# Weight sums of the seven-product units in a page of their own, and another order of the second run

## The chip, the cores and the metric

The kernel runs on one core of a Trainium2 chip. Five engines work side by side and wait for each other through semaphores: PE (TensorE: matmuls, and the loads of their stationary operand, PEld), DVE (VectorE), ACT (ScalarE), POOL (GpSimd) and SP (SyncE, which here issues most of the DMAs). The metric is the device time of one launch in microseconds (us). Lower is better.

## The reference

One layer of a hybrid encoder on 256 tokens of width 2048, in float32:

```
n = rms_norm(h); u = n @ W_in
a = MLA(u)                              (16 heads)
s = rms_norm((BiSSD(u)) * silu(z)) @ w_o_ssd       (K = 4096)
h = h + (sigmoid(g_a) * a + sigmoid(g_s) * s) @ W_out
h = h + (silu(gate) * val) @ ffn_w_down            (K = 5632), gate|val = conv(rms_norm(h) @ ffn_w_up)
out = rms_norm(h)
```

Two of its products matter here: that with `w_o_ssd` and that with `ffn_w_down`.

## The kernel before

**Jobs and half slabs.** All weights stream through one list of jobs. A job has a slab of 16 blocks of 128x128 (1 MB), loaded by one DMA into one of three `raw` buffers (L123; `load` is called two jobs ahead), and is used in half slabs. Since a float32 product is made of three products of rounded halves, each half slab is split: ACT copies it, rounded, into `wh` (L147, L190), and DVE subtracts that from the original into `wl` (L148, L191). There are five buffers of each (`HB=5`). Before PE uses half slab n, `ahead` (L1438) has `split_to` (L170) issue the splits through half slab n + 4, so splits run about five half slabs ahead of the matmuls.

**Seven-product units.** In most of the two products, two column groups, two token groups and two blocks of K form a 2x2 by 2x2 block product. Plain jobs take eight block products; a unit marked "seven" takes seven (`SEVEN`, L906), from sums of the activations (made once) and sums of the weights (made in the unit). With three matmuls of 512 columns each, a plain unit of the runs has 24 matmuls and a seven-product unit 21. A seven-product unit has four half slabs (`nh = 4`), and `split_seven` (L150) makes each of them:

- h = 0: B11 and B21, as they are;
- h = 1: T1 = B11 + B12 and T3 = B22 + B12, written over B11 and B12 in the slab (L159, L160), and then split;
- h = 2: T1 + B22 written over B11 (L163); B22 and that sum are split, each with its own copy and subtraction;
- h = 3: that sum + B21 written over B21 (L167), and then split (a half of the usual size).

So a seven-product unit has four adds of 128x512 on DVE and five copy/subtract pairs, two of 128x1024 and three of 128x512.

**Where they stand.** `os_run` (L916) makes the product with `w_o_ssd` in two runs, one for each half of the output columns; each run goes over 16 pairs of K blocks in an order that is written out by hand (L1331; S marks a seven-product unit): run 0 has four sevens, run 1 has six. At the end of a run, `inner` (L934) combines four of the sums after the last seven, and `outer` (L945) the rest. `mix_in` (L987) then gates and scales a run's result and adds it to the attention's part, which `mix_load` (L983) brings back from HBM; `mix_channels` (L994) transposes it on PE for the product with `W_out`. Those of run 0 are hung by `at(slot, ...)` to jobs of run 1 (L1346 to L1350): what hangs at a slot is issued before that job's matmuls. In the FFN, the first two of three parts of the down product have five seven-product units each, with a plain down job behind each (`L1384` to L1387).

**Order.** The text gives each engine's order only as a priority: the program is put into its final order when it is built, and an instruction that is ready may come before one that stands ahead of it in the text and is not. [...]

**Pages.** Larger intermediate tiles are pages of 4 KB per partition, from one pool of 29 (`page`, L77; `NPG=29`); a new page waits until one is free.

Of the kernel before, what the change touches and what calls it, by code (L numbers as in the profile page):

```python
# [15 lines left out]
P = 128  # L16
# [48 lines left out]
def tile_bidir_hybrid_layer(ctx: ExitStack, tc, xT, pos, vec, cst, w_in, w_r, w_v, w_qk, w_oa,  # L65
# [9 lines left out]
    act, dve, pe = nc.scalar, nc.vector, nc.tensor  # L75

    def page(shape, dt=F32, name="pg"):  # L77
        return pp.tile(shape, dt, tag="pg", bufs=NPG, name=name)
# [10 lines left out]
    def f32(ap):  # L89
        return ap.bitcast(F32)  # L90
# [55 lines left out]
    def hilo(wh, wl, v):  # L146
        act.activation(wh, v, AF.Copy)  # L147
        dve.tensor_sub(wl, v, f32(wh))  # L148

    def split_seven(i, h, wh, wl):  # L150


        r = raws[i].rearrange("p (m k) c -> p m k c", m=8)
        B11, B12, B21, B22 = r[:, :4, 0, :], r[:, 4:, 0, :], r[:, :4, 1, :], r[:, 4:, 1, :]
        if h == 0:
            vh, vl = (w.rearrange("p (k m) c -> p m k c", k=2) for w in (wh, wl))
            hilo(vh, vl, r[:, :4])
        elif h == 1:
            dve.tensor_add(B11, B11, B12)  # L159
            dve.tensor_add(B12, B22, B12)  # L160
            hilo(wh, wl, r[:, :, 0, :])
        elif h == 2:
            dve.tensor_add(B11, B11, B22)  # L163
            hilo(wh[:, :4, :], wl[:, :4, :], B22)
            hilo(wh[:, 4:, :], wl[:, 4:, :], B11)
        else:
            dve.tensor_add(B21, B11, B21)  # L167
            hilo(wh[:, :4, :], wl[:, :4, :], B21)

    def split_to(n):  # L170
        while hptr[0] < min(n, len(halves)):
            i, h, nb = halves[hptr[0]]
            wh = wp.tile([P, 8, P], F32R, tag="wh", bufs=HB, name="wh")
            wl = wp.tile([P, 8, P], F32R, tag="wl", bufs=HB, name="wl")
            if jobs[i].seven:
                split_seven(i, h, wh, wl)
                hl[hptr[0]] = (wh, wl)
                hptr[0] += 1
                continue
            if jobs[i].wide:  # L180
                r = raws[i].rearrange("p (m k) c -> p m k c", m=8)[:, 4 * h:4 * h + 4]
                vh, vl = (w.rearrange("p (k m) c -> p m k c", k=2) for w in (wh, wl))
            elif jobs[i].quad:

                r = raws[i].rearrange("p (m k) c -> p m k c", m=4)[:, :, 2 * h:2 * h + 2, :]
                vh, vl = (w.rearrange("p (k m) c -> p m k c", k=2) for w in (wh, wl))
            else:
                r = raws[i][:, 8 * h:8 * h + nb, :]
                vh, vl = wh[:, :nb, :], wl[:, :nb, :]
            act.activation(vh, r, AF.Copy)  # L190
            dve.tensor_sub(vl, r, f32(vh))  # L191
            hl[hptr[0]] = (wh, wl)
            hptr[0] += 1
# [793 lines left out]
    def mix_in(q, res):  # L987
        g = mixT[q] = mixS[q]
        for t in range(2):
            o = res[t, q % 2]  # L990
            dve.scalar_tensor_tensor(o, ts_[q][:, t, :], 1.0, o, ALU.add, ALU.mult)
            dve.scalar_tensor_tensor(g[:, t, :], o, r_ssd["t"][:, t:t + 1], g[:, t, :], ALU.mult, ALU.add)
# [212 lines left out]
    def at(slot, fn, *a):  # L1205
        late.append((slot, lambda: fn(*a)))
# [97 lines left out]
    for g in range(G):  # L1304
        b = len(jobs)
# [22 lines left out]
    b = len(jobs)  # L1328
    for g in range(G):
        at(b - 2 + g, ssd_split, g)  # L1330
    runs = "0 1 2 3 4 5 8 S10 9 S11 6 S14 7 S15 12 13", "0 1 2 3 4 S6 5 S7 8 S10 9 S11 12 S14 S15 13"  # L1331
    runs = [[(int(w.lstrip("S")), w[0] == "S") for w in r.split()] for r in runs]
    done = {}

# [10 lines left out]
    at(b + 17, ssd_r)  # L1345
    for q in range(2):  # L1346
        at(b + 17 + q, mix_load, q)
        at(b + 19 + q, lambda q: mix_in(q, done[0]), q)
        at(b + 20 + q, mix_channels, q)
        at(b + 25 + q, mix_load, 2 + q)  # L1350
    b = len(jobs)
    cells = [{} for _ in range(4)]
# [11 lines left out]
    b = len(jobs)  # L1364
# [115 lines left out]
    i = 0  # L1480
# [112 lines left out]
```

## Time and profile before

| | us |
|---|---|
| median of three runs | 1960.38 |
| lowest and highest run | 1959.31, 1964.65 |
| profiled execution | 1959.09 |
| its span, first to last instruction | 1957.3 |
| PE, PEld, DVE, ACT busy in the span | 1937.9, 1688.1, 1562.7, 1240.4 |
| mean granted clock of PE | 0.998 of full speed |

The runs of the product with `w_o_ssd` lie between 935 and 1117 us of the span, the seven-product units of the FFN between 1394 and 1454 and between 1660 and 1721 us.

A line of the timeline has the start, the duration, the engine, the line of the source, the operation, the tiles it writes and reads with their shapes, and a count where several were merged; square brackets hold the engine's idle time before it and what ended that. A row of the windows view has a stretch, its length, and the busy time and count of instructions of each engine, then PE's clock, the busy share of the DMA engines and GB/s. In the runs, the matmuls are at L931; in the FFN, those of the plain jobs at L217 and L224 and those of the sevens at L1098 to L1100.

### The profile page before, as it was taken

Reading aid. Unit: us, or ns where it says so; the run is one execution under the profiler, and the core shown is the slowest. Engines: PE = TensorE matmul, PEld = TensorE weight load, DVE = VectorE, ACT = ScalarE, POOL = GpSimd, SP = SyncE. Lnnn points to the kernel's source line nnn. Section 1 sums busy time; section 2 is a strip of 40 time slices with the busy share of each in tenths; the row PEclk is TensorE's granted clock in tenths of the full one; section 3 lists DMA queues with packets and bytes.
Section 4 is the critical chain, followed back from the end, with each engine's and each line's share of the span. In section 5 each row is a group of like instructions: output and inputs, shape, how many; then the busy total and the mean of one; then the engine's idle time right before and its main releaser. Section 6 shows DMA issues by size and latency. Waiting matters only on the chain.

```text
span 1957.3 us, 28870 instructions
## 1 busy us (share of the span) xinstructions
PE 1937.9 (99%) x10948; PEld 1688.1 (86%) x10948; DVE 1562.7 (80%) x2583; ACT 1240.4 (63%) x1975; POOL 16.2 (1%) x36
## 2 busy tenths in 40 slices
PE   9999999999999999999999999999999999999997
PEld 8899988888888888888878788888888888888887
DVE  8887765779879878879887886887887887887775
ACT  6566544778888988978554554656455565555563
POOL 0200000000000000000000000000000000000000
PEclk9999999999999999999999999999999999999999
DMA  7654457665565566565466575555456554464553
GB/s 287 199 166 147 141 175 222 240 234 171 201 234 191 195 217 205 186 216 189 153 212 213 168 265 183 183 178 209 160 175 225 178 209 173 172 215 173 202 169 124
DMA packets 118906, 379.55 MB, mean 194 GB/s; under 512 B 9712, under 2 KB 53168, under 8 KB 90864
## 3 DMA queue, kind: packets, MB, share of 16 engines
q1 hardware_dynamic: 116976, 375.09, 56.0%
q0 software_dynamic: 1024, 1.54, 0.3%
q8 instruction: 86, 1.41, 0.3%
q10 hardware_dynamic: 768, 1.09, 0.2%
q14 instruction: 52, 0.43, 0.1%
HBM read 372.08 MB, written 4.42 MB: 192 GB/s over the span
## 4 chain that ended last, share of the span: by engine, by line
PE 90%; DVE 6%; ACT 2%; DMA 1%; issue 1%; SPq 0%; ACTq 0%; DVEq 0%
PE g L217 39%; PE g L224 20%; PE g L931 6%; PE g L252 4%; PE g L253 4%; PE g L254 4%; DVE wl L191 2%; DVE wl L148 1%; PE s L931 1%; PE g L196 1%; PE g L198 1%; PE g L197 1%; ACT wh L190 1%; PE s L836 1%; PE s L845 1%
## 5 line engine op out<-in xcount | busy, mean ns | idle before, releaser
L191 DVE TENSOR_TENSOR wl<-raw,wh 128x1024 fp32r<-128x1024 f32 (+1 forms) x634 | 753.2, 1202 | 202.2 <-ACT wh L190 127.5
L190 ACT ACTIVATE wh<-raw 128x1024 fp32r<-128x1024 f32 (+1 forms) x634 | 651.4, 1038 | 276.4 <-PE g L217 102.2
L217 PE MATMUL g<-xHL,wh 128*128 128x512 f32 x1424 | 341.6, 392 | 0.2 <-DVE cu L267 0.2
L217 PE MATMUL g<-hHL,wh 128*128 128x512 f32 x1408 | 327.8, 390 | 0.0
L217 PEld LDWEIGHTS g<-xHL,wh 128*128 128x128 f32 x1424 | 262.5, 188 | 52.1 <-PE s L198 0.4
L217 PEld LDWEIGHTS g<-hHL,wh 128*128 128x128 f32 x1408 | 261.5, 188 | 52.4
L224 PEld LDWEIGHTS g<-xHL,wl 128*128 128x128 f32 x1424 | 182.6, 191 | 6.9
L224 PE MATMUL g<-xHL,wl 128*128 128x256 f32 x1424 | 184.7, 283 | 0.0
L224 PEld LDWEIGHTS g<-hHL,wl 128*128 128x128 f32 x1408 | 174.8, 192 | 3.4
L224 PE MATMUL g<-hHL,wl 128*128 128x256 f32 x1408 | 176.0, 283 | 0.0
L147 ACT ACTIVATE wh<-raw 128x512 fp32r<-128x512 f32 (+1 forms) x100 | 78.2, 798 | 101.5 <-DVE raw L160 53.5
L217 PE MATMUL g<-aHL,wh 128*128 128x512 f32 x532 | 129.2, 393 | 0.7
L1048 DVE SCALAR_TENSOR_TENSOR uc<-u,V,uc 128x255 f32<-128x255 f32 x176 | 84.9, 482 | 56.3 <-ACT uc L1046 54.6
L931 PE MATMUL g<-wh,yHL 128*128 128x512 f32 x392 | 125.6, 391 | 0.3 <-DVE m L948 0.3
L1046 ACT ACTIVATE uc<-u,V 128x256 f32<-128x256 f32 x88 | 52.3, 594 | 115.8 <-DVE u L274 115.8
L217 PEld LDWEIGHTS g<-aHL,wh 128*128 128x128 f32 x532 | 98.3, 188 | 24.5 <-ACT wh L190 4.2
L148 DVE TENSOR_TENSOR wl<-raw,wh 128x512 fp32r<-128x512 f32 (+1 forms) x100 | 88.5, 902 | 26.5 <-ACT wh L147 22.0
L252 PE MATMUL g<-wh,xHL 128*128 128x512 f32 x256 | 100.2, 391 | 0.0
L253 PE MATMUL g<-wl,xHL 128*128 128x512 f32 x256 | 99.9, 390 | 0.0
L254 PE MATMUL g<-wh,xHL 128*128 128x512 f32 x256 | 99.6, 389 | 0.0
L931 PEld LDWEIGHTS g<-wh,yHL 128*128 128x128 f32 x392 | 73.5, 188 | 16.0 <-issue 0.7
L931 PE MATMUL g<-wl,yHL 128*128 128x512 f32 x196 | 76.9, 393 | 1.3 <-DVE wl L191 1.3
(373 smaller groups left out, 2845.0 us busy)
## 6 DMA issues: line engine op xcount, KB each, us to landing
raw<-in_w_in SPq DMA_DIRECT2D x88, 1024.0 KB, 4.9
raw<-in_w_up SPq DMA_DIRECT2D x88, 1024.0 KB, 4.9
raw<-in_w_in SPq DMA_DIRECT2D x128, 256.0 KB, 3.8
raw<-in_w_os SPq DMA_DIRECT2D x32, 1024.0 KB, 6.1
raw<-in_w_dn SPq DMA_DIRECT2D x26, 1024.0 KB, 5.0
raw<-in_w_oa SPq DMA_DIRECT2D x64, 256.0 KB, 4.0
FB<-acsD SPq DMA_DIRECT2D x32, 512.0 KB, 7.8
raw<-in_w_out SPq DMA_DIRECT2D x12, 1024.0 KB, 6.0
```

The source lines that it names most:

```text
L147: act.activation(wh, v, AF.Copy)
L148: dve.tensor_sub(wl, v, f32(wh))
L190: act.activation(vh, r, AF.Copy)
L191: dve.tensor_sub(vl, r, f32(vh))
L217: pe.matmul(ps, lhsT=wh[:, b, :], rhs=x, start=k == 0, stop=False)
L224: pe.matmul(cell["ps"][:, 0, :], lhsT=wl[:, b, :], rhs=get(k)[:, 0, :], start=False, stop=k == ktot - 1)
L252: pe.matmul(ps, lhsT=x[:, 0, ts], rhs=wH[:, kk, :], start=k == 0, stop=False)
L253: pe.matmul(ps, lhsT=x[:, 0, ts], rhs=wL[:, kk, :], start=False, stop=False)
L254: pe.matmul(ps, lhsT=x[:, 1, ts], rhs=wH[:, kk, :], start=False, stop=k == kt - 1)
L931: pe.matmul(M[nm], lhsT=x, rhs=w, start=left[nm] == total[nm], stop=left[nm] == 1)
L1046: act.activation(o, u, AF.Identity, scale=vcol("fcw", 88 + cb), bias=vcol("fcb", cb))
L1048: dve.scalar_tensor_tensor(o[:, a], u[:, b], vcol("fcw", k * 88 + cb), o[:, a], ALU.mult, ALU.add)
```

## The change

`split_seven` makes T1 and T3 with the first half slab, behind its split, in a page of their own, `T13`. The second half slab is split from that page, through the same rearranged views of `wh` and `wl` as the first. Behind its split stand both running sums: T1 + B22 goes over B12, and that sum plus B21 over B21. The third and last half slabs are then split from the slab with no add of their own. The number of adds, copies and subtractions stays.

In run 1 the seven-product units stand between plain ones: S6 comes one place earlier, and 12 stands between S14 and S15. `mix_in` and `mix_channels` for run 0's result are hung one job earlier; `mix_load` stays.

```diff
+    sums = {}
+
     def split_seven(i, h, wh, wl):
...
         if h == 0:
             vh, vl = (w.rearrange("p (k m) c -> p m k c", k=2) for w in (wh, wl))
             hilo(vh, vl, r[:, :4])
+            t = sums[i] = page([P, 2, 4, P], name="T13")
+            dve.tensor_add(t[:, 0], B11, B12)
+            dve.tensor_add(t[:, 1], B22, B12)
         elif h == 1:
-            dve.tensor_add(B11, B11, B12)
-            dve.tensor_add(B12, B22, B12)
-            hilo(wh, wl, r[:, :, 0, :])
+            t = sums.pop(i)
+            vh, vl = (w.rearrange("p (k m) c -> p m k c", k=2) for w in (wh, wl))
+            hilo(vh, vl, t)
+            dve.tensor_add(B12, t[:, 0], B22)
+            dve.tensor_add(B21, B12, B21)
         elif h == 2:
-            dve.tensor_add(B11, B11, B22)
             hilo(wh[:, :4, :], wl[:, :4, :], B22)
-            hilo(wh[:, 4:, :], wl[:, 4:, :], B11)
+            hilo(wh[:, 4:, :], wl[:, 4:, :], B12)
         else:
-            dve.tensor_add(B21, B11, B21)
             hilo(wh[:, :4, :], wl[:, :4, :], B21)
...
-    runs = "0 1 2 3 4 5 8 S10 9 S11 6 S14 7 S15 12 13", "0 1 2 3 4 S6 5 S7 8 S10 9 S11 12 S14 S15 13"
+    runs = "0 1 2 3 4 5 8 S10 9 S11 6 S14 7 S15 12 13", "0 1 2 3 S6 4 S7 5 S10 8 S11 9 S14 12 S15 13"
...
-        at(b + 19 + q, lambda q: mix_in(q, done[0]), q)
-        at(b + 20 + q, mix_channels, q)
+        at(b + 18 + q, lambda q: mix_in(q, done[0]), q)
+        at(b + 19 + q, mix_channels, q)
```

More of the change, by code (lines that the diff above doesn't have):

```diff
@@ L157, in split_seven @@
             hilo(vh, vl, r[:, :4])
+            t = sums[i] = page([P, 2, 4, P], name="T13")
+            dve.tensor_add(t[:, 0], B11, B12)
+            dve.tensor_add(t[:, 1], B22, B12)
         elif h == 1:
-            dve.tensor_add(B11, B11, B12)
-            dve.tensor_add(B12, B22, B12)
-            hilo(wh, wl, r[:, :, 0, :])
+            t = sums.pop(i)
+            vh, vl = (w.rearrange("p (k m) c -> p k m c", k=2) for w in (wh, wl))
+            hilo(vh, vl, t)
+            dve.tensor_add(B12, t[:, 0], B22)
+            dve.tensor_add(B21, B12, B21)
         elif h == 2:
-            dve.tensor_add(B11, B11, B22)
             hilo(wh[:, :4, :], wl[:, :4, :], B22)
-            hilo(wh[:, 4:, :], wl[:, 4:, :], B11)
+            hilo(wh[:, 4:, :], wl[:, 4:, :], B12)
         else:
-            dve.tensor_add(B21, B11, B21)
             hilo(wh[:, :4, :], wl[:, :4, :], B21)
```

## Prediction

> **What bounds the kernel now.** I read the page's busy shares first, then its chain of waits.
>
> ```profile
> span 1957.3 us, 28870 instructions
> PE 1937.9 (99%) x10948; PEld 1688.1 (86%) x10948; DVE 1562.7 (80%) x2583; ACT 1240.4 (63%) x1975; POOL 16.2 (1%) x36
> PE 90%; DVE 6%; ACT 2%; DMA 1%; issue 1%; SPq 0%; ACTq 0%; DVEq 0%
> ```
>
> PE is busy for 99% of the span, so nearly everywhere the matmuls set the pace. Only what DVE and ACT hold of the chain, 8%, can be had by better splits, and only as far as PE really stood still in it. So I looked for stretches of PE that take longer than the same matmuls take elsewhere. The windows view, restricted to the matmul line of the two output-projection runs, gives the norm of a plain unit (24 matmuls) and, for all engines, of a seven-product unit (21); the chain in order of time gives it for the FFN's jobs.
>
> ```profile
> 955.56:961.00 5.44, 5.44 (x25) 4.50 (x24) 1.00 0.60 185
> 987.52:992.28 4.76, 4.76 (x22) 3.94 (x21) 4.35 (x7) 3.69 (x5) 0.00 (x0) 1.00 0.11 33
> 1231.59 7.28 PE g L217 x32
> 1238.87 3.83 PE g L224 x32
> ```
>
> A plain unit is 5.44 us, a seven-product unit 4.76 us; two 16-block FFN jobs take 7.28 + 3.83 = 11.11 us, one 5.56. (The counts in brackets include a matmul that hangs over from the unit before.) Against these norms stand the units around the sevens: first run 0, then run 1, then periods of the FFN (a seven-product unit and a plain down job; two first and the last of eight), each cut from one PE start to the next.
>
> ```profile
> 1002.48:1008.50 6.02, 5.73 (x25) 4.43 (x24) 1.00 0.93 287
> 1013.31:1019.52 6.21, 5.73 (x26) 4.43 (x24) 1.00 0.88 265
> 1091.23:1097.47 6.24, 5.74 (x25) 4.42 (x24) 1.00 0.92 281
> 1102.27:1110.99 8.72, 6.26 (x23) 3.55 (x21) 1.00 0.36 123
> 1110.99:1117.00 6.01, 5.99 (x25) 4.16 (x23) 1.00 0.65 196
> 1408.68:1419.98 11.30, 10.93 (x56) 8.70 (x55) 9.78 (x13) 5.75 (x9) 0.00 (x0) 1.00 0.55 188
> 1419.98:1431.24 11.26, 10.92 (x55) 8.70 (x54) 9.79 (x14) 5.71 (x8) 0.00 (x0) 1.00 0.55 185
> ...
> 1709.24:1720.46 11.22, 11.00 (x56) 8.71 (x55) 11.16 (x15) 7.68 (x11) 0.00 (x0) 1.00 0.27 86
> ```
>
> **The sum of what can be recovered.** Run 0: (6.02 - 5.44) + (6.21 - 5.44) = 1.35 us. Run 1: 12 loses 0.80, S15, which stands directly behind S14, loses 8.72 - 4.76 = 3.96, and 13 loses 0.57: 5.3 us. FFN: a period should be 4.76 + 5.56 = 10.32 us and takes 11.26; there are four such periods in each of the two parts that have sevens (all eight lie between 11.22 and 11.30), so 8 x 0.93 = 7.4 us. Together 14.1 us, 0.7% of the span. No change to the splits can bring more.
>
> Who makes PE wait there shows in the DVE timeline of one FFN period, with ACT's second half slab behind it and then the marks of a period in run 1:
>
> ```profile
> 1404.86 1.22 DVE L148 TENSOR_TENSOR wl<-raw,wh 128x1024 fp32r<-128x1024 f32 x1
> 1406.11 0.69 DVE L159 TENSOR_TENSOR raw<-raw 128x512 f32<-128x512 f32 x1
> 1406.84 0.69 DVE L160 TENSOR_TENSOR raw<-raw 128x512 f32<-128x512 f32 x1
> 1408.74 1.83 DVE L148 TENSOR_TENSOR wl<-raw,wh 128x1024 fp32r<-128x1024 f32 x2 [1.21 <-ACT wh L147]
> 1410.48 0.69 DVE L163 TENSOR_TENSOR raw<-raw 128x512 f32<-128x512 f32 x1
> 1411.09 0.42 DVE L1159 TENSOR_TENSOR h<-h,g 128x256 f32<-128x256 f32 x1
> 1411.42 0.69 DVE L167 TENSOR_TENSOR raw<-raw 128x512 f32<-128x512 f32 x1
> 1412.02 0.69 DVE L148 TENSOR_TENSOR wl<-raw,wh 128x512 fp32r<-128x512 f32 x1
> ...
> 1412.95 0.69 DVE L148 TENSOR_TENSOR wl<-raw,wh 128x512 fp32r<-128x512 f32 x1
> 1413.83 2.36 DVE L191 TENSOR_TENSOR wl<-raw,wh 128x1024 fp32r<-128x1024 f32 x2 [0.19 <-ACT wh L190]
> 1416.11 1.22 DVE L148 TENSOR_TENSOR wl<-raw,wh 128x1024 fp32r<-128x1024 f32 x1
> ```
> ```profile
> 1407.65 1.58 ACT L147 ACTIVATE wh<-raw 128x1024 fp32r<-128x1024 f32 x2 [3.20 <-DVE raw L160]
> ```
> ```profile
> 1071.04 1.22 DVE L148 TENSOR_TENSOR wl<-raw,wh 128x1024 fp32r<-128x1024 f32 x1
> ...
> 1074.92 1.83 DVE L148 TENSOR_TENSOR wl<-raw,wh 128x1024 fp32r<-128x1024 f32 x2 [1.21 <-ACT wh L147]
> ...
> 1079.81 2.36 DVE L191 TENSOR_TENSOR wl<-raw,wh 128x1024 fp32r<-128x1024 f32 x2 [0.26 <-ACT wh L190]
> 1082.08 1.22 DVE L148 TENSOR_TENSOR wl<-raw,wh 128x1024 fp32r<-128x1024 f32 x1
> ```
>
> The pattern repeats from 1404.86 to 1416.11: 11.25 us, the period of PE. In it DVE stands idle twice, 1.21 and 0.19 us. So DVE, not PE, sets the period: 11.25 - 1.40 = 9.85 us of DVE work against 10.32 us of PE work, and the 1.21 us pushes it over. It is a round trip: the sums at L159 and L160 overwrite the slab that the first half slab's copy and subtraction read, so they come behind that subtraction; ACT can copy the second half slab only after them; DVE has nothing else and waits for the copy. In run 1 the DVE pattern is 11.04 us long (from 1071.04 to 1082.08) with idle times of 1.21 and 0.26, so 9.57 us of work against 4.76 + 5.44 = 10.20 of PE.
>
> **The change part by part.** *Operations.* Before and after, a unit has four adds of 128x512 and five copy/subtract pairs. The adds move: T1 and T3 go to a page of their own at the first half slab, the two running sums to the second. Nothing is added to ACT, PE or the queues. T1 and T3 no longer write what the first half slab reads; they need only the landed slab and a free page. Of two dependent adds the starts lie 0.73 apart (L159 to L160), of independent ones of this size less:
>
> ```profile
> 1051.19 1.28 DVE L148 TENSOR_TENSOR wl<-raw,wh 128x512 fp32r<-128x512 f32 x2
> ```
>
> Two take 1.28, the second adding 0.59. T1 and T3 are independent, so DVE saves about 0.12 us a unit; 20 units, 2.4 us of DVE time, none of it on PE's path by itself. [...]
>
> *The round trip.* If T1 and T3 stand on DVE before the first subtraction, ACT copies first and second half slab back to back, and the second subtraction follows the first with no idle time. DVE then needs some 9.7 us in a period of 10.32, PE is late next, and the period falls to PE's. Where they land is not told by the source: the rows show that issue order is not text order (L163 stands behind a subtraction of its own half slab that the text has after it; L1159, the evacuation of the job before, stands between), so an instruction that is ready fills a gap. T1 and T3 are ready once the slab is there:
>
> ```profile
> 1404.97 0.38 SPq L135 DMA_DIRECT2D raw<-in_w_dn  x1
> raw<-in_w_dn SPq DMA_DIRECT2D x26, 1024.0 KB, 5.0
> raw<-in_w_os SPq DMA_DIRECT2D x32, 1024.0 KB, 6.1
> ```
>
> The slab issued at 1404.97 is there some 5.0 us later, at 1410, and its first subtraction runs at 1416.11: 6 us in which a gap can take the sums. Once PE sets the pace, splits wait for PE to free a wh/wl buffer, and DVE has 10.32 - 9.7 = 0.6 us idle a period plus the 1.2 us that the two sums no longer take behind the first subtraction. I therefore take it that they go early: between ends of 0 (same place, same idle) and 0.93 us a period, 0.85, which is 8 x 0.85 = 6.8 us. Run 0, whose order stays, has the same round trip: 1.0 of its 1.35.
>
> *The second half slab's adds* stand behind its subtraction; ACT's copy of T1 + B22 waits for one, that of the last half slab for both. Behind ACT's waiting copy stand only copies of later half slabs, and before the change it waits for adds in the same way (L163, L167).
>
> *The order of run 1.* S14 12 S15 in place of 12 S14 S15: no two sevens adjoin. Adjacent, they want 2 x (9.57 - 2.28) = 14.6 us of DVE (2.28 being a plain unit's two subtractions, 1413.83 to 1416.11) against 9.5 of PE; that is S15's 3.96. Apart, each pair needs 9.6 of 10.20. With the round trip gone I take 4.8 of the 5.3 us.
>
> *One slot earlier.* S6, mix_in and the transposes all move up one job, into the first plain units of run 1. What DVE has left there:
>
> ```profile
> 1032.00:1037.40 5.40, 5.40 (x25) 4.40 (x25) 3.39 (x5) 2.99 (x5) 0.00 (x0) 1.00 0.90 243
> 1037.40:1042.80 5.40, 5.40 (x25) 4.48 (x24) 3.49 (x5) 2.12 (x2) 0.00 (x0) 1.00 0.95 346
> 1039.31 0.75 DVE L992 SCALAR_TENSOR_TENSOR mixS<-m,rtok,mixS 128x512 f32<-128x512 f32 x1 [2.15 <-DMA mixS<-mixD]
> ```
>
> DVE is idle for 2.01 + 1.91 = 3.9 us in two units, and S6 brings 7.3 - 2.3 = 5.0 us more work into a slot that was plain. Behind mix_in's wait for its DMA (2.15 us) DVE's later splits are queued, and PE's transposes wait for mix_in. The five half slabs that are split ahead absorb most of 1.1 us; between 0 and 2 us I take 0.7 lost. The DMAs of mix_load keep their slots. The page is one of 29 and lives for one half slab; should none be free, T1 waits and the case is the first rival.
>
> *Sum:* 6.8 + 1.0 + 4.8 - 0.7 = 11.9 us; I take 11.4, since DVE would run at 94% and must catch up after each disturbance. The profiled execution took 1959.09 us (span 1957.3, 1.8 around it), so it would be 1947.7. The median of the runs shown, 1960.38, is 1.3 above it: **1949.0 us**.
>
> **The rivals.** *(a) The sums stay behind the first subtraction.* Nothing but their text moves: first subtraction, T1, T3, then the same wait of 1.2 us for ACT. For it speaks that the text has them there and that in the pattern DVE goes from L191 to the first subtraction without a gap. Against it speaks the 6 us of readiness and the 0.19 to 0.26 us gap inside them. Then FFN gains 8 x 0.15 = 1.2 us, run 0 0.3, run 1 only by its order: DVE's 10.9 a pair against 10.2 over six pairs, 4.2 us, less a stock of about 2.5 (the four pairs before lost 0.8 of 4 x 0.84), so 1.7 lost in place of 5.3. About 5 us: 1955.4, no change that can be told. [...]
>
> *(b) The sums stand too early: slower.* If T1 is put on DVE behind the first running sum of the unit before, 1.25 + 1.14 + 0.72 = 3.1 us after the slab's load is issued, DVE waits 5.0 - 3.1 = 1.9 us in the FFN and 3.0 in the runs, with the subtractions of the unit before queued behind it, as L992 shows for another transfer. [...] DVE's pattern is then 9.7 + 1.9 = 11.6 against 11.25, 8 x 0.35 = 3 us lost, and in the runs 9.5 + 3.0 = 12.5 against 11.04, which over nine pairs less the stock already there is 5 to 9 us: about 1969. It decides from a wait of 1.4 us, the idle time that goes. Against it: at that point the subtractions themselves are ready and stand first.
>
> *(c) Run 1 gains nothing.* S6 comes into the mix work, DVE never catches up at 9.6 of 10.2, and the 4.8 - 0.7 is not had: 6.8 + 1.0 = 7.8 less 0.5, 1953.1.
>
> **How the numbers follow.** Forecast 0.58, (a) 0.25, (b) 0.09, (c) 0.08. About 0.3%, 5.9 us, is what a measurement of this kernel can tell from no change: the limits are 1954.5 and 1966.3. Faster: 0.57 of the forecast, 0.06 of (c), 0.03 of (a): 0.66. Slower: 0.08, nearly all of (b). Within: 0.26. Range: below, all 14.1 us and a little scatter, 1945.5; above, (a) with 2 us more, 1957.5. It leaves out (b) and the far ends, under 0.2.
>
> **What would show it.** Right: in the FFN the starts of T1 and T3 stand before the first subtraction; the idle time before the second is near 0; the period on PE is 10.3 to 10.4; DVE shows gaps that end with PE. S15's window falls to about 4.8. Wrong: 1.2 us before the second subtraction still there (a); a DVE wait that ends with a DMA of raw before T1 (b); windows over 5.5 us in run 1 from S6 on (c). The prediction fails as a whole if DVE, once freed, finds another wait of a microsecond a period that the trace of before hides behind this one.

## The result and the profile after

| | before | after |
|---|---|---|
| median, us (runs of one comparison) | 1959.91 (four, 1959.31 to 1964.65) | 1944.13 (four, 1943.88 to 1944.84) |
| ratio, 95% interval | | 0.9915 [0.9898, 0.9932] |
| profiled execution, span, us | 1959.09, 1957.3 | 1944.84, 1943.1 |

The kernel became faster by 0.7 to 1.0%. That is a larger gain than was forecast (1949.0 us), and 1.4 us beyond the lower end of the range. The first lines of the page of the changed kernel, and its chain of waits:

```profile
span 1943.1 us, 28860 instructions
PE 1928.8 (99%) x10948; PEld 1689.8 (87%) x10948; DVE 1556.6 (80%) x2583; ACT 1243.5 (64%) x1975; POOL 16.2 (1%) x36
PE 97%; DVE 1%; ACT 1%; DMA 1%; issue 0%; SPq 0%; DVEq 0%; ACTq 0%
```

The counts of instructions on the five engines are the same. DVE's share of the chain went from 6 to 1%, PE's from 90 to 97%. (One thing is put wrongly ahead of the prediction, in the text and in the diff: the second half slab has a rearranged view of its own, `p (k m) c -> p k m c`, where the first has `p m k c`.)

Line numbers behind `split_seven` are 5 higher than before: L190 is now L195, L191 is L196, L931 is L936; T1 and T3 are made at L161 and L162, the running sums T1 + B22 and the last one at L167 and L168. The windows view of the changed kernel, for run 0's 12, run 1's 12, S15 and 13, and one FFN period of each part (columns as before: length, then PE, PEld, DVE, ACT):

```profile
1012.97:1018.41 5.44, 5.44 (x26) 4.50 (x25) 5.44 (x7) 2.71 (x3) 0.00 (x0) 1.00 0.92 269
1094.14:1099.58 5.44, 5.44 (x26) 4.50 (x24) 5.00 (x7) 2.30 (x4) 0.00 (x0) 1.00 0.37 101
1099.58:1104.34 4.76, 4.76 (x23) 3.94 (x21) 3.00 (x3) 4.41 (x6) 0.00 (x0) 1.00 0.34 110
1104.34:1109.78 5.44, 5.44 (x26) 4.50 (x24) 5.44 (x8) 1.64 (x2) 0.00 (x0) 1.00 0.75 236
1411.98:1422.31 10.33, 10.33 (x55) 8.87 (x54) 9.20 (x14) 5.92 (x7) 0.00 (x0) 1.00 0.60 205
1674.84:1685.17 10.33, 10.33 (x55) 8.87 (x54) 9.36 (x13) 5.92 (x7) 0.00 (x0) 1.00 0.60 205
```

Every one of them stands at PE's norm: 5.44, 4.76, and 4.76 + 5.56 = 10.32. PE is busy for the whole of each stretch, while DVE's share goes from 3.00 of 4.76 us to 5.44 of 5.44. The DVE timeline of one FFN period of the changed kernel shows where the sums went:

```profile
1410.97 0.69 DVE L161 TENSOR_TENSOR T<-raw 128x512 f32<-128x512 f32 x1 [0.45 <-DMA raw<-in_w_dn]
1411.58 0.68 DVE L148 TENSOR_TENSOR wl<-raw,wh 128x512 fp32r<-128x512 f32 x1
1412.18 0.69 DVE L162 TENSOR_TENSOR T<-raw 128x512 f32<-128x512 f32 x1
...
1414.58 0.69 DVE L167 TENSOR_TENSOR raw<-T,raw 128x512 f32<-128x512 f32 x1
1415.19 1.22 DVE L196 TENSOR_TENSOR wl<-raw,wh 128x1024 fp32r<-128x1024 f32 x1
1416.32 1.22 DVE L148 TENSOR_TENSOR wl<-raw,wh 128x1024 fp32r<-128x1024 f32 x1
1417.46 1.22 DVE L148 TENSOR_TENSOR wl<-T,wh 128x1024 fp32r<-128x1024 f32 x1
1418.59 0.69 DVE L168 TENSOR_TENSOR raw<-raw 128x512 f32<-128x512 f32 x1
...
1421.61 0.69 DVE L161 TENSOR_TENSOR T<-raw 128x512 f32<-128x512 f32 x1 [1.13 <-DMA raw<-in_w_dn]
```

T1 and T3 run 4 to 5 us before the first subtraction (1416.32), T1 even ahead of the last subtraction of the unit before (1411.58). The first running sum comes before the first subtraction too, and the second subtraction follows the first without a gap. What DVE waits for now is the slab itself, 0.45 and 1.13 us ahead of T1: the wait of rival (b), which does no harm in this stretch. ACT, in the same stretch of the changed kernel, waits for PE to give back a buffer:

```profile
1413.63 1.06 ACT L195 ACTIVATE wh<-raw 128x1024 fp32r<-128x1024 f32 x1 [2.25 <-PE s L1105]
1414.98 1.06 ACT L147 ACTIVATE wh<-raw 128x1024 fp32r<-128x1024 f32 x1 [0.29 <-PE s L1105]
```

The view that sums the waits by line (total us, times, longest) has the round trip as one row, the subtractions of the sevens (L148) waiting for ACT's copy. Before:

```profile
DVE wl L148 <- ACT wh L147: 22.0, 20, 1.2
```

After, with the two new waits for slabs:

```profile
DVE T L161 <- DMA raw<-in_w_os: 5.8, 5, 1.9
DVE T L161 <- DMA raw<-in_w_dn: 3.9, 5, 1.1
DVE wl L148 <- ACT wh L147: 2.5, 3, 1.1
```

20 waits with a longest of 1.2 us became three. Where the time came from, by the starts of PE's matmuls in the two traces:

| stretch | before | after | difference |
|---|---|---|---|
| up to run 0 | 935.33 | 935.61 | +0.28 |
| run 0 | 90.08 | 88.24 | -1.84 |
| run 1 | 91.59 | 85.93 | -5.66 |
| from there to the second seven of FFN part 1 | 291.68 | 291.88 | +0.20 |
| to the second seven of part 2 | 266.76 | 262.86 | -3.90 |
| to the end of PE's last matmul | 272.95 | 269.62 | -3.33 |

Together -14.25 us, which is also the difference of the two profiled executions.

### The profile page after: what moved, and what is told of

Its sections match the earlier page's. It is cut to its first block, busy times and chain, and to the rows that moved or that the text cites. A ratio compares the mean times of both kernels' runs of the same rounds, so it can differ in the third digit from the quotient of the medians.

```text
span 1943.1 us, 28860 instructions
## 1 busy us (share of the span) xinstructions
PE 1928.8 (99%) x10948; PEld 1689.8 (87%) x10948; DVE 1556.6 (80%) x2583; ACT 1243.5 (64%) x1975; POOL 16.2 (1%) x36
## 4 chain that ended last, share of the span: by engine, by line
PE 97%; DVE 1%; ACT 1%; DMA 1%; issue 0%; SPq 0%; DVEq 0%; ACTq 0%
PE g L222 41%; PE g L229 21%; PE g L936 7%; PE g L257 5%; PE g L258 4%; PE g L259 4%; PE s L936 1%; PE g L201 1%; PE g L203 1%; PE g L202 1%; PE s L222 1%; PE s L841 1%; PE s L850 1%; PE s L201 0%; PE s L203 0%; PE s L202 0%
## 5 line engine op out<-in xcount | busy, mean ns | idle before, releaser
L196 DVE TENSOR_TENSOR wl<-raw,wh 128x1024 fp32r<-128x1024 f32 (+1 forms) x634 | 754.5, 1201 | 207.4 <-ACT wh L195 127.7
L195 ACT ACTIVATE wh<-raw 128x1024 fp32r<-128x1024 f32 (+1 forms) x634 | 654.9, 1039 | 317.0 <-PE g L222 109.6
L936 PE MATMUL g<-wh,yHL 128*128 128x512 f32 x392 | 125.0, 390 | 0.0
L936 PEld LDWEIGHTS g<-wh,yHL 128*128 128x128 f32 x392 | 73.6, 188 | 15.2
L147 ACT ACTIVATE wh<-raw 128x1024 fp32r<-128x1024 f32 (+1 forms) x80 | 56.9, 733 | 38.0 <-PE g L936 13.3
L936 PE MATMUL g<-wl,yHL 128*128 128x512 f32 x196 | 76.3, 389 | 0.0
L229 PEld LDWEIGHTS g<-aHL,wl 128*128 128x128 f32 x532 | 67.9, 191 | 2.4
```

Source lines behind the costliest of these rows:

```text
L229: pe.matmul(cell["ps"][:, 0, :], lhsT=wl[:, b, :], rhs=get(k)[:, 0, :], start=False, stop=k == ktot - 1)
L936: pe.matmul(M[nm], lhsT=x, rhs=w, start=left[nm] == total[nm], stop=left[nm] == 1)
```

## The experiments

The first question was which of the two parts of the change did it. One kernel took the new split alone, the other the new order and slots alone.

**Split alone.**

```diff
-    runs = ..., "0 1 2 3 S6 4 S7 5 S10 8 S11 9 S14 12 S15 13"
+    runs = ..., "0 1 2 3 4 S6 5 S7 8 S10 9 S11 12 S14 S15 13"
-        at(b + 18 + q, lambda q: mix_in(q, done[0]), q)
-        at(b + 19 + q, mix_channels, q)
+        at(b + 19 + q, lambda q: mix_in(q, done[0]), q)
+        at(b + 20 + q, mix_channels, q)
```

> Only the new split (page T13, running sums at the second half slab); order of run 1 and the slots of mix_in and mix_channels as before the change. Before 1959.9 us, changed 1944.1. Theory A (the round trip alone makes PE wait; S15 shows what backlog four pairs had built up): FFN 7.1 us, run 0 1.9 us and most of run 1's 5.6 us are gained, about 1945 to 1946; S15's stretch on PE below 5.5 us. Theory B (two adjoining sevens are a cost of their own): S15 still takes 7 to 8.7 us and the time is 1948 to 1950.

Measured: 1945.24 us (1945.11 to 1945.62), ratio 0.9926 [0.9911, 0.9941]. Windows of this kernel, for 12, S14 and S15 of run 1, the two sevens side by side:

```profile
1089.01:1094.83 5.82, 5.73 (x25) 4.43 (x24) 5.82 (x8) 2.31 (x4) 0.00 (x0) 1.00 0.49 147
1094.83:1099.59 4.76, 4.76 (x22) 3.94 (x21) 4.69 (x7) 3.71 (x5) 0.00 (x0) 1.00 0.47 155
1099.59:1104.35 4.76, 4.76 (x22) 3.94 (x21) 4.76 (x7) 4.13 (x6) 0.00 (x0) 1.00 0.25 61
```

S15 stands directly behind S14 and takes 4.76 us, where it took 8.72 before. DVE is busy nearly throughout (4.69 and 4.76 of 4.76), yet PE does not wait in the sevens; the 12 ahead of them loses 0.38 us. So two adjoining sevens cost nothing by themselves; before the change they came on top of the backlog that the sevens before them had built up.

**Order and slots alone** (the old `split_seven` put back).

```diff
         if h == 0:
             hilo(vh, vl, r[:, :4])
-            t = sums[i] = page([P, 2, 4, P], name="T13")
-            dve.tensor_add(t[:, 0], B11, B12)
-            dve.tensor_add(t[:, 1], B22, B12)
         elif h == 1:
+            dve.tensor_add(B11, B11, B12)
+            dve.tensor_add(B12, B22, B12)
...
```

> Only the order of run 1 and the slots of mix_in and mix_channels; the split as before the change. Theory A: the round trip stays, DVE's pattern stays 11.0 us a pair against 10.2 on PE; FFN and run 0 gain nothing, run 1 gains 2 to 4 us because no two sevens adjoin: 1956 to 1958. Theory B: run 1 gains all of its 5.6 us: 1954.3.

Measured: 1958.01 us (1957.49 to 1958.55), ratio 0.999 [0.9981, 1.0]. Run 1 is 89.64 us long, 1.95 less than before; the FFN's periods stay at 11.2 to 11.3. Windows of this kernel for 9, S15 and 13 of run 1:

```profile
1086.72:1092.96 6.24, 5.73 (x25) 4.43 (x24) 4.96 (x6) 3.04 (x4) 0.00 (x0) 1.00 0.89 267
1104.01:1108.98 4.97, 4.97 (x22) 3.86 (x21) 4.63 (x8) 3.60 (x7) 0.00 (x0) 1.00 0.22 89
1108.98:1114.83 5.85, 5.85 (x25) 4.35 (x24) 5.85 (x8) 2.56 (x3) 0.00 (x0) 1.00 0.66 202
```

S15's own loss is nearly gone, but the plain units from 9 on still lose 0.4 to 0.8 us each, and S6, one place earlier, takes 6.26 us where it took 5.06. The order spreads the lack of DVE time; it does not remove it. Beside the new split, order and slots are worth 1.1 us (1945.24 against 1944.13). Of that 0.38 us lies in run 1. Behind run 1, in the kernel with the split alone, PE waits 0.45 us for `mixS` and 0.34 for `mHL`, tiles of the mix work that DVE makes; the changed kernel has neither wait.

**Which of the split's moves?** It makes three at once: T1 and T3 into a page, T1 and T3 early, the running sums early. In the next kernel T1 and T3 keep their page but are held at their place in the text, behind the first subtraction, which is rival (a) as the prediction told it.

```diff
-            dve.tensor_add(t[:, 0], B11, B12)
-            dve.tensor_add(t[:, 1], B22, B12)
+            tc.keep_in_program_order(dve.tensor_add(t[:, 0], B11, B12))
+            tc.keep_in_program_order(dve.tensor_add(t[:, 1], B22, B12))
```

> The changed kernel, with T1 and T3 held on DVE behind the first half slab's subtraction, where rival (a) of the prediction has them. Theory A (the gain needs the sums to go ahead of the first subtraction): 1.2 us of idle time before the second subtraction comes back, FFN periods of 11.0 us, 1950 to 1953. Theory C (the running sum that stands there now fills part of the wait): idle time of 0.6 us or less, DVE about 10.2 us a period, FFN periods of 10.3 to 10.5, 1944 to 1946.

Measured: 1944.31 us (1943.31 to 1944.91), ratio 0.992 [0.9905, 0.9935]: nothing is lost. Its DVE timeline, one unit of the FFN:

```profile
1406.07 1.22 DVE L148 TENSOR_TENSOR wl<-raw,wh 128x1024 fp32r<-128x1024 f32 x1
1407.22 0.68 DVE L161 TENSOR_TENSOR T<-raw 128x512 f32<-128x512 f32 x1
1407.82 0.68 DVE L162 TENSOR_TENSOR T<-raw 128x512 f32<-128x512 f32 x1
1408.54 0.69 DVE L167 TENSOR_TENSOR raw<-T,raw 128x512 f32<-128x512 f32 x1
1409.26 0.69 DVE L168 TENSOR_TENSOR raw<-raw 128x512 f32<-128x512 f32 x1
1409.87 1.22 DVE L148 TENSOR_TENSOR wl<-T,wh 128x1024 fp32r<-128x1024 f32 x1
```

ACT still copies T only after both sums (from 1408.62 here, after 2.58 us in which it waited for T3), but DVE is not idle meanwhile: the two running sums, 0.72 + 0.61 us from start to start, fill the 1.2 us. Before, T1 + B22 was written over B11, which the second half slab's copy and subtraction still had to read, so it could not stand there.

**The text of T1 and T3 at the second half slab**, one half slab later:

```diff
-            t = sums[i] = page([P, 2, 4, P], name="T13")
         elif h == 1:
-            t = sums.pop(i)
+            t = page([P, 2, 4, P], name="T13")
+            dve.tensor_add(t[:, 0], B11, B12)
+            dve.tensor_add(t[:, 1], B22, B12)
```

> The changed kernel, with T1 and T3 made in their page in the text of the second half slab, not of the first. Theory A (what counts is that they no longer overwrite the slab, so they go where there is a gap, whatever their place in the text): DVE order and time as the changed kernel, 1944 +- 1. Theory D (the half slab of lead in the text is what brings the gain): they stand behind the first subtraction, 1.2 us idle, 1950 or more.

Measured: 1945.30 us (1944.73 to 1945.35), ratio 0.9925 [0.991, 0.994]. T1 and T3 stand on DVE in the same gaps as in the changed kernel, and the FFN's periods are 10.33. It is some 1 us slower than the changed kernel. Of that, the two profiled executions (1945.35 and 1944.84) show 0.5. PE waits 0.52 us here, until 1651.44, for another tile of the FFN (`aHL`, copied by ACT and subtracted by DVE), where the changed kernel does not wait. The sums have a part in it: ACT's copy ends at 1650.60, but T1, which waited 0.21 us for its slab, stands on DVE from 1650.36, and the subtraction for `aHL` comes behind it at 1650.97. The rest of the wait is not explained.

**No page for T1 and T3.** They go over the slab as before; only T1 + B22 gets a page, so that both running sums can run while ACT makes the second half slab's copy.

```diff
         elif h == 1:
-            t = sums.pop(i)
-            hilo(vh, vl, t)
-            dve.tensor_add(B12, t[:, 0], B22)
-            dve.tensor_add(B21, B12, B21)
+            dve.tensor_add(B11, B11, B12)
+            dve.tensor_add(B12, B22, B12)
+            hilo(wh, wl, r[:, :, 0, :])
+            t = sums[i] = page([P, 4, P], name="R")
+            dve.tensor_add(t, B11, B22)
+            dve.tensor_add(B21, t, B21)
```

> The changed kernel with the page on the other side: T1 and T3 overwrite the slab as before the change, and the running sum T1 + B22 goes to a page, so that both running sums may run while ACT copies T1 and T3. Theory C (two adds that fill DVE's wait for ACT are enough, whichever they are): no idle time over 0.3 us before the second subtraction, FFN periods of 10.3 us, 1944 to 1946. Theory A (T1 and T3 must be free to go ahead of the first subtraction): 1.2 us idle, FFN periods of 11.0, 1950 to 1953.

Measured: 1944.37 us (1944.17 to 1944.77), ratio 0.9922 [0.9907, 0.9937]. FFN periods 10.33, and on DVE again subtraction, T1, T3, both running sums, second subtraction, with no idle time between. So neither a page for T1 and T3 nor their early place is needed. It was enough here that DVE had something that may run while ACT copies.

**The running sums late.** T1 and T3 in their page and free; the running sums held at the places in the text that they had before.

```diff
-            dve.tensor_add(B12, t[:, 0], B22)
-            dve.tensor_add(B21, B12, B21)
         elif h == 2:
+            tc.keep_in_program_order(dve.tensor_add(B12, sums.pop(i)[:, 0], B22))
...
         else:
+            tc.keep_in_program_order(dve.tensor_add(B21, B12, B21))
```

> The changed kernel with T1 and T3 in their page and free, but each running sum held where it stood before the change (in front of the third and the last half slab's subtractions). Theory A (early T1 and T3 are enough by themselves): FFN periods of 10.3, 1944 to 1946. If the gain came from the running sums alone: 1.2 us idle, 1950 or more.

Measured: 1948.52 us (1948.15 to 1949.29), ratio 0.9943 [0.9928, 0.9958]. This lies between the two expectations: run 0 is 89.25 and run 1 88.61 us long, longer than after the change, but the FFN's periods are 10.33. In this kernel's DVE timeline some units have the old wait and some have none; one with it:

```profile
1411.82 0.68 DVE L162 TENSOR_TENSOR T<-raw 128x512 f32<-128x512 f32 x1
1413.71 1.23 DVE L148 TENSOR_TENSOR wl<-T,wh 128x1024 fp32r<-128x1024 f32 x1 [1.21 <-ACT wh L147]
```

Where T3 happens to come late, nothing else is there to fill the wait.

**Both held**: the two edits above together, T1 and T3 behind the first subtraction and the running sums late.

> The changed kernel with both held: T1 and T3 behind the first subtraction, the running sums in front of the third and last half slab's. This is rival (a) of the prediction with its idle time. Theories A and C alike: 1.2 us idle is back before the second subtraction, DVE 9.7 + 1.2 = 10.9 us a period, FFN periods of 10.9 to 11.1 (5 to 6 us), run 0 and run 1 together 1 to 3 us: 1950 to 1953. If it stays at 1944 to 1946, the idle time was never the cause.

Measured: 1966.67 us (1965.36 to 1968.68), ratio 1.0038 [1.0024, 1.0052], slower than before the change and far above the 1950 to 1953 that were expected. Its DVE timeline over one FFN period:

```profile
1408.56 0.68 DVE L162 TENSOR_TENSOR T<-raw 128x512 f32<-128x512 f32 x1
1410.45 1.22 DVE L148 TENSOR_TENSOR wl<-T,wh 128x1024 fp32r<-128x1024 f32 x1 [1.21 <-ACT wh L147]
...
1415.19 0.69 DVE L148 TENSOR_TENSOR wl<-raw,wh 128x512 fp32r<-128x512 f32 x1 [0.44 <-ACT wh L147]
1416.14 2.36 DVE L196 TENSOR_TENSOR wl<-raw,wh 128x1024 fp32r<-128x1024 f32 x2 [0.26 <-ACT wh L195]
```

The same adds, copies and subtractions, and idle times of 1.21, 0.44 and 0.26 us: its periods are 11.55 to 11.91. It is held harder than the kernel before, where the last running sum moved freely; the 0.44 is from that, since ACT's last copy waits for this sum (1.58 us, until 1414.53). Against the kernel that holds T1 and T3 alone (1944.31), the only difference is that the running sums come late, and it costs 22.4 us. Against the kernel with T1 and T3 in the slab and the running sums beside ACT's copy, 22.3 us lie in nothing but where four adds stand and what they write over.

**The page alone, nothing held.** T1 and T3 as in the changed kernel, the running sums at their old places in the text, free to move.

```diff
-            dve.tensor_add(B12, t[:, 0], B22)
-            dve.tensor_add(B21, B12, B21)
         elif h == 2:
+            dve.tensor_add(B12, sums.pop(i)[:, 0], B22)
...
         else:
+            dve.tensor_add(B21, B12, B21)
```

> T1 and T3 in a page of their own at the first half slab, as in the changed kernel; the two running sums stand in the text where they stood before the change (T1 + B22 at the third half slab, the last one at the fourth), but are not held there. Theory C (what counts is that the running sums do not wait for a copy of ACT, and an instruction that is ready may come ahead of its place in the text): they go early by themselves, 1944.3 us as the changed kernel, FFN periods of 10.33. Rival (their place in the text holds them, as in the kernel before, where T1 + B22 came behind its half slab's subtraction): as where they were pinned there, 1948.5 us, with waits of 1.21 us of DVE for ACT in some units.

Measured: 1947.05 us (1946.38 to 1947.74), ratio 0.9932 [0.9919, 0.9946], between the two. The running sums do go early in most units; L148's waits for ACT are 3.8 us in all, and run 0 and the FFN's periods are as fast as after the change. What is lost lies at two places. PE waits 1.07 us for `aHL`, until 1654.31, ahead of the second part's sevens; T1 stands in front of that subtraction too, and delays it by 0.6. The larger loss is one unit of run 1, the plain 9, which takes 7.30 us. The DVE timeline of this kernel there (L168 is T1 + B22 here):

```profile
1082.52 0.69 DVE L161 TENSOR_TENSOR T<-raw 128x512 f32<-128x512 f32 x1 [4.10 <-DMA raw<-in_w_os]
1083.13 0.68 DVE L162 TENSOR_TENSOR T<-raw 128x512 f32<-128x512 f32 x1
1083.85 0.69 DVE L168 TENSOR_TENSOR raw<-T,raw 128x512 f32<-128x512 f32 x1
1084.46 2.35 DVE L196 TENSOR_TENSOR wl<-raw,wh 128x1024 fp32r<-128x1024 f32 x2
```

and PE:

```profile
1085.73 0.50 PE L936 MATMUL g<-wl,yHL 128*128 128x512 f32 x1 [1.57 <-DVE wl L196]
```

This is rival (b), shown: T1 stands first on DVE and waits 4.10 us for its slab, and behind it are the two subtractions at L196 that PE needs; ACT's copies for them had ended at 1080.31 and 1081.68, and they ran from 1084.46. The slab was issued at 1073.64, about as in the changed kernel (1073.19), but took 8.9 us to land in place of 6.7. The load before it had been issued 2.0 us later (1070.04 against 1068.03), so that more of the two overlap; that this is the reason is argued, not shown.

**How much room has DVE?** T1 is made three times in each unit, two more adds, 1.2 us.

```diff
             dve.tensor_add(t[:, 0], B11, B12)
+            dve.tensor_add(t[:, 0], B11, B12)
+            dve.tensor_add(t[:, 0], B11, B12)
```

> The changed kernel with two more adds of 128x512 on DVE in each seven-product unit (T1 is made three times over), 1.2 us. If DVE is what comes next behind PE, with 9.7 us of work in an FFN period of 10.32: 10.9 us, 8 x 0.6 = 5 us lost in the FFN, 0 to 3 us in the runs (9.4 + 1.2 = 10.6 against 10.2): 1949 to 1952. If there is more room than that: 1944 to 1946.

Measured: 1948.22 us (1947.48 to 1948.76), ratio 0.9941 [0.9926, 0.9956]. 20 units x 1.2 = 24 us more DVE work cost 4.1 us, between what the two theories had expected. A window of this kernel over one FFN period:

```profile
1404.22:1414.55 10.33, 10.33 (x56) 8.87 (x54) 10.23 (x15) 5.03 (x7) 0.00 (x0) 1.00 0.62 204
```

DVE is busy for 10.23 of 10.33 us and the period is still PE's. Run 0 is 90.06 us, 1.8 longer than after the change: there DVE also has `BiSSD` and `inner` to do. Run 1 is 86.02. The other 2 us lie mostly around the FFN's periods, not in them: from the second seven of part 1 to that of part 2 this kernel takes 1.35 us longer, and PE waits there 0.57 us for `aHL` and 0.24 for `h`, tiles that DVE makes as well.

**More seven-product units.** If PE sets the pace, each further seven-product unit should save three matmuls, 5.44 - 4.76 = 0.68 us. Three kernels tried it, in the FFN, in run 0, and in both:

```diff
-    NU = 5
+    NU = 6
...
```
```diff
-    runs = "0 1 2 3 4 5 8 S10 9 S11 6 S14 7 S15 12 13", ...
+    runs = "0 1 2 3 4 5 S10 8 S11 9 S14 S15 12 S6 S7 13", ...
```

> The changed kernel with six seven-product units in place of five in each of the two FFN parts that have them. A seven-product unit saves three matmuls of 512 columns against a plain one, 5.44 - 4.76 = 0.68 us. Theory A (PE sets the pace now, DVE has 10.33 - 9.7 = 0.6 us to spare in a period): all of it is had, 2 x 0.68 = 1.4 us less, 1942.8 us, periods on PE still 10.33. Theory B (DVE's spare time at the end of a part is already used up by the stock of split half slabs): a sixth unit loses about a microsecond to DVE, 1944 us or a little more.

> The changed kernel with six seven-product units in place of four in run 0 of the product with w_o_ssd (order 0 1 2 3 4 5 S10 8 S11 9 S14 S15 12 S6 S7 13). Theory A (PE sets the pace): 2 x 0.68 = 1.4 us less, 1942.8 us, run 0 86.9 us long in place of 88.2. Theory B (run 0's DVE has other work beside the splits; 1.2 us more in each of four units, 4.8 us, already made it 1.8 us longer, so some 3 us are to spare, and two more units bring 2 x 5.0 us): 5 to 7 us of DVE work too many, less the stock; run 0 gets longer than 88.2, 1946 to 1950 us.

> Both: six seven-product units in each FFN part and six in run 0. Theory A: 4 x 0.68 = 2.7 us less than the changed kernel, 1941.4 us. Theory B: the sum of what the two show alone.

Measured, beside 1960.12 before:

| | us | ratio, interval |
|---|---|---|
| six in the FFN | 1943.13 (1942.87 to 1943.97) | 0.9915 [0.9901, 0.9929] |
| six in run 0 | 1944.90 (1944.57 to 1945.68) | 0.9924 [0.9912, 0.9937] |
| both | 1943.28 (1942.96 to 1943.88) | 0.9916 [0.9902, 0.9929] |

In the FFN the first theory holds: all its periods are 10.33, and the stretches from the second seven of part 1 to that of part 2 and on to PE's last matmul are 262.31 and 268.35 us, together 1.82 less than after the change (1.36 from the matmuls; the rest is not explained). The median is 1.0 us below the changed kernel's; the intervals of the ratios cannot tell the two apart, the traces can. In run 0 neither holds. It is 87.81 us long, 0.43 less than after the change: not the 1.36 of the first theory, and not longer, as the second has it. Run 1 behind it takes 0.67 us more, so nothing is won, and the time lies between the two theories'. Two gaps of PE make up most of the loss, here in the PE timeline of that kernel:

```profile
1014.86 0.50 PE L936 MATMUL s<-wl,ySh 128*128 128x512 f32 x1 [0.64 <-DVE wl L148]
1027.85 0.73 PE L936 MATMUL g<-wh,yHL 128*128 128x512 f32 x2 [0.43 <-ACT wh L195]
```

Both together bring 1943.28 us, not the 1941.4 of the first theory; the two taken alone would add up to 1943.9.

## Why the prediction was right or wrong

**What bounds the kernel: right.** The round trip was the cost. Among the kernels with the same operations and the new order of run 1, L148's total wait for ACT is 2.2 to 3.8 us where the time is 1944.1 to 1947.1, 13.7 at 1948.5 and 30.5 at 1966.7; in the kernel before it is 22.0.

**The ceiling: right, in part by luck.** 14.1 us were to be had; the two profiled executions differ by 14.25. The parts agree less well than the sum. The unit 13 of run 0, 5.89 us before and 5.44 after, was not in the list: 0.45 us. Run 1 gave 5.66 in place of 5.3, and the FFN 7.0 in place of 7.4.

**The sum: here the prediction failed.** The step is "6.8 + 1.0 + 4.8 - 0.7 = 11.9 us; I take 11.4". Each gain was taken below its full size and came in full or nearly so, and the two costs did not come:

| term | forecast | measured |
|---|---|---|
| FFN | 6.8 | 7.0 (3.90 + 3.33 - 0.20) |
| run 0 | 1.0 | 1.84 |
| run 1, with S6 and the mix work one slot earlier | 4.8 - 0.7 | 5.66 |
| to catch up after disturbances | -0.5 | 0 |

That is 3.1 us short (14.5 against 11.4), 1.6 of it in run 1 and 0.8 in run 0. The mechanism was right, the sizes were not: once DVE's need in a period fell below PE's, the period went all the way to PE's; it was 10.33 us with DVE busy for 9.20 us and for 10.23 alike. That DVE at 94% "must catch up after each disturbance" was wrong; with two more adds a unit it ran at 99% in the FFN's periods and PE still did not wait in them. S6's earlier slot, taken at 0.7, cost nothing either: run 1's stretch from 0 through S6 and 4 took 35.06 us before and 34.93 after. With the old split S6 did lose 1.2 us in that slot, so it is the new split that makes it free. (The slots and S6's place were not tried apart.)

**The base.** 1949.0 starts from the median of three runs, 1960.38, while the sum was made against the profiled execution, 1959.09: 1.3 us more. Profile against profile the sum gave 1947.7, and 1944.84 came; the median after lies another 0.7 below. The low end of the range, 1945.5, was the full 14.1 us off 1960.38 with a little scatter, so a full gain and this base together missed it. Medians of before in later comparisons are 1959.91 to 1960.12.

**Where the sums go: right, but not what decides.** T1 and T3 do stand ahead of the first subtraction. Held behind it, they cost nothing. The early place is one way to end the wait in most units; the freed running sums are another, and either alone gives the FFN its period. For the runs it takes the running sums: with early T1 and T3 alone, 4.4 us are missing.

**Rival (a): its mechanism fell.** "First subtraction, T1, T3, then the same wait of 1.2 us" came only when the running sums were held as well. In the change as written, the text itself allows the running sums into the gap: they read T and the slab and no longer overwrite what ACT copies. The prediction saw that they move and looked only at who waits for them. As told it would have been 1944.3, not 1955.4; with the running sums held it is 1966.7.

**Rival (b): its wait exists, its price was wrong.** T1 waits up to 1.9 us for its slab after the change, and in the runs and the FFN's periods PE loses nothing; "it decides from a wait of 1.4 us" left out that DVE has idle time of its own (1.13 of 10.33 us in the FFN period above) and that the splits are some five half slabs ahead. Only at one place does the changed kernel pay for it, ahead of the sevens of FFN part 1, where what stands behind T1 is not a split but `aHL`, which PE needs at once. The rows are from the DVE timeline, then from PE's:

```profile
1386.97 0.69 DVE L161 TENSOR_TENSOR T<-raw 128x512 f32<-128x512 f32 x1 [0.81 <-DMA raw<-in_w_dn]
1387.59 0.42 DVE L1071 TENSOR_TENSOR aHL<-uc,aHL 128x256 fp32r<-128x256 f32 x1
```
```profile
1388.06 0.73 PE L222 MATMUL g<-aHL,wh 128*128 128x512 f32 x2 [0.45 <-DVE aHL L1071]
```

ACT's copy for `aHL` ended at 1386.62; the subtraction came 0.97 us later, behind T1, and PE waited 0.45. With the running sums at their old places a wait of T1 of 4.10 us stopped PE for 1.57.

The work queued behind such a wait, which this rival took from the row of L992, shows in two more rows of the trace of before, from ACT's timeline and from DVE's:

```profile
1037.57 1.06 ACT L190 ACTIVATE wh<-raw 128x1024 fp32r<-128x1024 f32 x1 [1.66 <-PE g L931]
```
```profile
1039.98 1.22 DVE L191 TENSOR_TENSOR wl<-raw,wh 128x1024 fp32r<-128x1024 f32 x1
```

The copy ended at 1038.63, while DVE waited for L992's transfer until 1039.31; the subtraction of that half slab came behind L992, 1.35 us after its copy.

**The order of run 1.** That two adjoining sevens want 14.6 us of DVE against 9.5 of PE was not by itself the cause of S15's 3.96: with the new split the two adjoining sevens run at 4.76 each. Order and slots give 0.4 us of run 1 (86.31 against 85.93), and 1.95 with the old split.

**The 0.12 us of independent adds: right.** With T1 and T3 behind each other in one timeline, as held above, T3 starts 0.60 us after T1, and the last running sum 0.72 after the one that it reads. Why the two distances differ, no run shows.

**Not seen:** a wait of T1 for a page. All its waits in the changed kernel end with the DMA of its slab.

## What to carry to other kernels

When two engines pass work back and forth, look for the one wait that recurs each period, and ask what else the waiting engine could do at that moment; here it was a later operation of the same unit that was kept out only because it overwrote an input. Writing that result elsewhere was worth more here than making the operation before it earlier (1944.3 against 1948.5 us). Once an engine's work per period is below that of the one that sets the pace, take the whole gain of that period into the forecast; here 9.20 and 10.23 us of DVE work in 10.33 both gave PE's period, with splits some five half slabs ahead. Price apart the stretches where that engine has other work: in run 0 and around the FFN's periods two more adds a unit did cost PE time.

## What the runs showed of the hardware that was not expected

DVE at 10.23 us of work in a period of 10.33 did not slow PE in that period, with half slabs split some five ahead. What a wait of DVE for a DMA costs depended on what stood behind it: 1.86 us ahead of splits, in run 1 of the changed kernel, cost PE nothing, 0.81 us ahead of `aHL` cost 0.45, and 4.10 us ahead of splits cost 1.57. A 1 MB load landed after 5.9 to 7.4 us between 1060 and 1095 us of the changed kernel, and after 6.0 to 8.9 in the kernel with the page alone; why it varies is not shown.
